# Hybrid decoder layer: later beta and decay products, later offers of two kinds of transposes, a residual transposed without its norm, and another clock for the planner's tasks

## The chip, the cores and the metric

The kernel runs on one core of one Trainium2 chip. The metric is the device time of one execution, in microseconds (us). The time before is a median of 981.6 us over three runs (980.06, 981.60 and 982.82).

## The reference, cut to what matters

One layer of a decoder over 512 tokens of width 1024, in float32: two token mixers side by side (retention and a gated delta rule), merged by gates, and then a gated feed-forward net with a causal convolution over three tokens.

```python
u = rmsnorm(h, g_mix)                                   # h: 512 x 1024
proj = u @ w_in                                         # 1024 x 9232
(rq, rk, rv, rgate, dq, dk_, dv_, dz, db, da, gate_r, gate_d) = split(proj)
...
g = -exp(dn_a_log) * softplus(da + dn_dt_bias)          # decay of each token and head
beta = sigmoid(db)                                      # step of the delta rule
do = gated_delta_chunkwise(cq, ck, cv, g, beta)         # 8 heads, chunks of 128 tokens
do = do * rsqrt(mean(do * do) + EPS) * dn_norm_g
y_dn = (do * silu(dz)) @ w_dn_br
merged = sigmoid(gate_r) * y_ret + sigmoid(gate_d) * y_dn
h = h + merged @ w_o

u2 = rmsnorm(h, g_ffn)                                  # (h * r) * g_ffn, one r per token
up = causal_dwconv(u2 @ w_up, ffn_conv_w) + ffn_conv_b  # 1024 x 5632, three taps
a, b = split(up, 2)
h = h + (silu(a) * b) @ w_down                          # 2816 x 1024
out = rmsnorm(h, g_final)
```

The factor r of the second rmsnorm belongs to a token. The products with w_up treat every token by itself, so r can be applied before them or after them; it has to be applied before the convolution, which mixes tokens.

## The kernel before, in words

**Numbers.** Every large product is made of three TensorE products in the fp32r type: each operand is split into a rounded part (hi) and the rest (lo), and hi·hi, lo·hi and hi·lo are summed (`mm3`, L387). ScalarE makes the hi part, VectorE the lo part (`weights`, L351, for a block of weights; `split`, L532, for an activation). The five square products of the mixer and the product with w_down go through Strassen's scheme in Winograd's form, with seven products of quarters in place of eight (`product`, L449; `PRODUCTS`, L62).

**Layout.** Activations that enter a product stand with channels on the 128 partitions and the 512 tokens in a row. Where a result has tokens on the partitions, TensorE transposes four 128x128 pieces of it into one PSUM bank against the identity (`transpose4`, L544).

**Order of the work.** TensorE's stream is written out by `body`, product by product. All else (evictions, norms, splits, transposes, the scans of the two mixers) is written as small tasks, Python generators. A class `Order` (L98 to L148) plans while the program is built: it has a clock, which every product moves on (`product`, L124), and for each other engine the time at which it is free (`issue`, L114). After each group of three products `poll` (L132) takes the tasks whose time has come, lets each issue its next step, and puts it back into the queue with a new time: the end of what it issued, plus a hop of 0.3 us (`HOP`), plus what the task itself yields. So a task that yields 0.6 is offered 0.6 us later than it could be. `hold` (L145) moves the clock on until something is planned to be ready. Each engine then runs its instructions strictly in the order in which this planner wrote them; semaphores keep the data right whatever the real times are. An instruction that comes too early in the order makes its engine wait, with everything that is queued behind it.

**Stages, in time.** (1) To 24 us: loading x, splitting it (`g_split`, L602), the squares of x for the first norm (`square`, `row_scales`, L615 to L649), and the first two weight blocks (`first_blocks`, L1257), which loop over eight k-tiles of 128 channels: three products into `pk`, three into `pq`, and two into `pba`, the 16 columns of w_in that give beta and the decays. `ba_w`, the split of those columns, is made by `ba_split` (L666). The norm of x is not applied to x: the products are scaled afterwards by `R`, a tile with the norm of each token in every partition (`scaled`, L1276). R comes from a product of ones with a diagonal tile (L637 to L646). `decays` (L708) makes beta and the decays from `pba`. (2) To 311 us: the products for keys, queries and values, with the fronts of the heads, retention, and the delta rule of heads 0 to 3. `solve_up` (L972) builds the inverses by small products, `scan` (L1026) runs over chunks, `scan_end` (L1080) norms the output of a head and transposes it (tile `pot`). (3) To 415 us: the products `pz` for the output gates, and the delta rule of heads 4 to 7. (4) To 578 us: four Strassen products (`matrix`, L1462): two gates, two branches. `m_out` (L1413) transposes the merged rows (tile `pmt`) and makes operands of them. (5) To 623 us: the product with w_o (`o_product`, L1555), whose results `o_into` (L1513) adds into the residual `h1`, eight tiles of 128x512. When both halves of a token tile are complete, it takes their squares on ScalarE, the sum on VectorE (`row_scale`, L526), the inverse root on GpSimd, and multiplies the two halves by it (one on ScalarE, one on VectorE, tile `hs`); `u2_out` and `u2_split` (L1537, L1544) transpose them (tile `pt`) and split them into u2hi and u2lo. (6) To 867 us: 44 blocks of w_up, alternately `pa` and `pb`; `ffn_conv` (L1574) reads each PSUM bank three times, once on ScalarE and twice on VectorE; `ffn_a` and `ffn_b` gate. The first three blocks run in halves, with tokens 256 to 511 first (`dense_c_halves`, L402). (7) To the end: the product with w_down (`down`, L1694), the last norm (`into`, L1659) and the output.

GpSimd issues the DMAs that add up weight quarters in memory (`presum`, L315), paced by a small pair of instructions on ScalarE and GpSimd (`pace`, L333). SyncE loads the weights (`fetch`, L288).

Of the kernel before, what the change touches and what calls it, by code (L numbers as in the profile page):

```python
# [19 lines left out]
P = 128  # L20
# [77 lines left out]
class Order:  # L98
# [15 lines left out]
    def issue(self, engine, us, banks=()):  # L114

        at = self.clock if self.now is None else self.now
        at = max(at, self.free.get(engine, 0.0))
        for b in banks:
            at = max([at, *(t + self.HOP for e, t in self.banks.get(b, {}).items() if e != engine)])
        self.done = self.free[engine] = at + us  # L120
        for b in banks:
            self.banks.setdefault(b, {})[engine] = self.done

    def product(self, us):  # L124
        self.clock += us
# [112 lines left out]
def body(nc, tc, ctx, io):  # L238
# [32 lines left out]
    def v3(ap, n=4):  # L271
        return ap.rearrange("p (n f) -> p n f", n=n)
# [807 lines left out]
    def scan_end(hd, o, ssqo):  # L1080
        h = hd["h"]
        ms = s4("mso")
        vec.tensor_scalar(ms, ssqo, 1.0 / P, EPS, ALU.mult, ALU.add)
        r = s4("ro")
        yield
        rsqrt(r, ms)
        yield
        vec.tensor_tensor(v3(o), v3(o), bc(r), ALU.mult)
        hd["got"].add("o")
        yield PW  # L1090
        pt = transpose4(o, "pot")
        yield
        d = S(f"doT{h}")
        act.activation(d, pt, AF.Identity, scale=prm[:, P_DG:P_DG + 1])
        doT[h] = d
# [158 lines left out]

    pba = PS("pba")

    def first_blocks():  # L1257

        pss = [PS(n) for n in ("pk", "pq")]
        ws = [tuple(v3(a, KT) for a in w) for w in first_w]  # L1260
        for k in range(KT):
            hold(lambda: k in g_ready)
            for i, ps in enumerate(pss):
                hold(lambda: (i, k // 4) in first_ready)
                mm3(ps, ws[i][0][:, k], ws[i][1][:, k], ghi[k], glo[k], k == 0, k == KT - 1)
                poll()
            hold(lambda: "ba" in first_ready)
            for j, x in enumerate(gx):
                pe.matmul(pba[:32], ba_w[:, k], x[k], start=(k + j == 0), stop=(k + j == KT))
            poll()  # L1270
        for i in range(2):
            spawn(weights(), 0.1 + 8.0 * i)
        spawn(decays(pba), 0.2)
        return pss
# [136 lines left out]
        o_opnd[name, t] = hi, lo  # L1411

    def m_out(t, i, r):  # L1413
        yield 0.2
        pt = transpose4(r, "pmt")
        yield
        name, half = f"B{i + 1}{t // 2 + 1}", t % 2
        m = o_raw[name, half] = S(f"mr{t}{i}")
        act.copy(m, pt)
        yield  # L1420
        if name != "B12":
            spawn(o_split(name, half, m))
        if name == "B12":
            t3 = S("mt3")
            vec.tensor_tensor(t3, o_raw["B22", half], m, ALU.subtract)
            t2 = o_raw["T2", half] = S("mt2")
            vec.scalar_tensor_tensor(t2, t3, -1.0, o_raw["B11", half], ALU.mult, ALU.subtract)
            spawn(o_split("T2", half, t2), 0.2)
            yield 0.5
            t1 = S("mt1")  # L1430
            vec.tensor_tensor(t1, o_raw["B11", half], m, ALU.subtract)
            spawn(o_split("T1", half, t1), 0.2)
            spawn(o_split("T3", half, t3), 0.2)
        elif name == "B21":
            while o_now[0] < 3:
                yield 0.5
            t4 = S("mt4")
            vec.scalar_tensor_tensor(t4, o_raw["T2", half], -1.0, m, ALU.mult, ALU.subtract)
            spawn(o_split("T4", half, t4), 0.2)
# [68 lines left out]

    u2hi = [S(f"u2hi{k}", F32R) for k in range(KT)]
    u2lo = [S(f"u2lo{k}", F32R) for k in range(KT)]  # L1510
    ssqs = [s4("ssq1", 2) for _ in range(NT)]

    def o_into(t, i, ps, op, last=False):  # L1513

        vec.tensor_tensor(h1[t][i], h1[t][i], ps, op)
        yield
        if not last:
            return
        junk = S("junk")
        act.activation(junk, h1[t][i], AF.Square, scale=1.0 / 32.0, accum_out=ssqs[t][:, i:i + 1])  # L1520
        if i == 0:
            return
        yield
        rr = s4("rr", 1)
        yield from row_scale(ssqs[t], rr)
        yield
        for i2 in range(2):
            xs = S("hs")
            if i2:
                vec.tensor_scalar(xs, h1[t][i2], rr, None, ALU.mult)  # L1530
            else:
                act.activation(xs, h1[t][i2], AF.Identity, scale=rr)
            spawn(u2_out(t, i2, xs), 0.6 * (i2 + 1))

    u2_ready = set()

# [35 lines left out]


    def ffn_conv(ps, ci):  # L1574
        w = prm[:, P_FW + 3 * ci:P_FW + 3 * ci + 3]
        acc = S2("acc")
        act.activation(acc, ps, AF.Identity, scale=w[:, 2:3], bias=prm[:, P_FB + ci:P_FB + ci + 1])
        yield
        for j in (1, 0):
            s = 2 - j  # L1580
            vec.scalar_tensor_tensor(acc[:, s:], ps[:, :T - s], w[:, j:j + 1], acc[:, s:], ALU.mult, ALU.add)
        yield
        return acc
# [215 lines left out]
```

## Time and profile before

| what | value |
|---|---|
| median of the runs | 981.6 us |
| the profiled execution: its own time | 980.2 us |
| its span, from the first to the last instruction | 978.3 us |
| outside the span | 1.9 us |
| mean granted TensorE clock | 0.999 |
| TensorE matmuls, busy | 963.4 us, 98% of the span |
| TensorE weight loads, busy | 804.6 us, 82% |
| VectorE, busy | 748.2 us, 76% |
| ScalarE, busy | 529.1 us, 54% |
| GpSimd, busy | 165.1 us, 17% |
| chain of work that ended last, TensorE's part | 85% |

In the profile's rows PE is TensorE's matmuls, PEld its weight loads, DVE VectorE, ACT ScalarE, POOL GpSimd and SP the engine that issues most DMAs. Most operations carry the line of a helper (L200 for all engines but TensorE, L230 and L235 for TensorE), so they are told apart by their tiles, written out<-in. A row of the timeline has the start and the duration in us, the engine, the operation, the tiles, the shape, and in brackets the idle time of the engine ahead of it with what ended it. A matmul of 512 columns shows 0.39 us, but the next one starts 0.23 us later, since matmuls overlap in the array; steps from start to start tell TensorE's pace. The pages' busy share of TensorE hides this overlap, so what matters is how long it stood idle, and for whom.

### The profile page before, as it was taken

How to read it: one execution, taken by the hardware profiler on the slowest of the kernel's cores; microseconds unless marked ns; L12 is line 12 of the kernel's file. 1: busy time of each engine (PE TensorE's matmuls, PEld its weight loads, DVE VectorE, ACT ScalarE, POOL GpSimd, SP SyncE). 2: the span in 40 equal slices, each digit the busy share in tenths (PEclk: the TensorE clock that was granted, in tenths of full speed). 3: DMA queues.
4: the chain of work that ended last, by engine and by line, in shares of the span. 5: the costliest groups of instructions: out<-in, count | busy, mean ns of one | idle time of the engine just before them, and what ended most of it. 6: DMA issues, size and time to landing. Idle time of an engine off the chain costs nothing.

```text
span 978.3 us, 14091 instructions
## 1 busy us (share of the span) xinstructions
PE 963.4 (98%) x5133; PEld 804.6 (82%) x5133; DVE 748.2 (76%) x1359; ACT 529.1 (54%) x1110; POOL 165.1 (17%) x209
## 2 busy tenths in 40 slices
PE   8999999999999999999999999899999999999997
PEld 6888888788888888978888887788888888888886
DVE  6888898567888898585899799865555676688785
ACT  6598222256955323586686646854344434356663
POOL 0121322224344020132000000221122221000001
PEclk9999999999999999999999999999999999999999
DMA  8244569958797695579976855666579998346663
GB/s 277 83 126 143 168 197 215 275 143 214 214 210 215 182 229 147 144 207 270 256 229 197 281 154 160 208 211 217 193 204 213 227 201 195 91 143 191 192 202 118
DMA packets 82949, 189.27 MB, mean 193 GB/s; under 512 B 22912, under 2 KB 31680, under 8 KB 82880
## 3 DMA queue, kind: packets, MB, share of 16 engines
q1 hardware_dynamic: 55360, 123.36, 39.4%
q0 software_dynamic: 27520, 65.02, 29.9%
q8 instruction: 40, 0.66, 0.3%
q14 instruction: 29, 0.24, 0.1%
HBM read 185.17 MB, written 68.19 MB: 259 GB/s over the span
## 4 chain that ended last, share of the span: by engine, by line
PE 85%; DVE 6%; ACT 4%; DMA 2%; issue 2%; POOL 0%; SPq 0%; POOLq 0%; DVEq 0%; ACTq 0%
PE pb L230 12%; PE pa L230 12%; PE py L230 12%; PE pd L230 10%; PE pz L230 9%; PE pr L230 9%; PE pq L230 3%; PE pv L230 3%; PE psc L230 3%; PE pk L230 3%; DVE wlo L200 2%; PE po L230 2%; PE pro L230 1%; ACT whi L200 1%; PE pm L230 1%
## 5 line engine op out<-in xcount | busy, mean ns | idle before, releaser
L200 ACT CAST whi<-wraw 128x1024 fp32r<-128x1024 f32 (+1 forms) x214 | 219.9, 1029 | 184.9 <-PE pr L230 54.2
L200 DVE TENSOR_TENSOR wlo<-wraw,whi 128x1024 fp32r<-128x1024 f32 (+1 forms) x214 | 255.3, 1194 | 63.7 <-ACT whi L200 63.1
L200 POOL TENSOR_SCALAR tock<-tick 128x1 f32<-128x1 f32 x72 | 34.0, 472 | 399.6 <-ACT tick L200 399.6
L200 DVE SCALAR_TENSOR_TENSOR acc<-pb,prm,acc 128x511 f32<-128x511 f32 (+1 forms) x44 | 33.0, 749 | 57.0 <-ACT acc L200 56.2
L230 PE MATMUL pa<-u2lo,whi 128*128 128x512 f32 (+1 forms) x192 | 71.4, 372 | 0.0
L230 PE MATMUL pa<-u2hi,whi 128*128 128x512 f32 (+1 forms) x192 | 71.4, 372 | 0.0
L230 PE MATMUL pa<-u2hi,wlo 128*128 128x512 f32 (+1 forms) x192 | 71.3, 371 | 0.0
L230 PE MATMUL pb<-u2hi,whi 128*128 128x512 f32 (+1 forms) x184 | 70.0, 380 | 0.0
L230 PE MATMUL pb<-u2lo,whi 128*128 128x512 f32 (+1 forms) x184 | 69.9, 380 | 0.0
L230 PE MATMUL pb<-u2hi,wlo 128*128 128x512 f32 (+1 forms) x184 | 69.9, 380 | 0.0
L230 PE MATMUL py<-whi,oh 128*128 128x512 f32 x160 | 62.9, 393 | 0.0
L230 PE MATMUL py<-wlo,oh 128*128 128x512 f32 x160 | 62.3, 390 | 0.0
L230 PE MATMUL py<-whi,ol 128*128 128x512 f32 x160 | 62.3, 389 | 0.0
L230 PE MATMUL pd<-whi,T 128*128 128x512 f32 (+1 forms) x198 | 55.3, 366 | 0.0
L230 PE MATMUL pz<-ghi,whi 128*128 128x512 f32 x128 | 51.4, 402 | 0.0
L230 PE MATMUL pr<-whi,ghi 128*128 128x512 f32 x128 | 51.1, 399 | 0.0
L230 PE MATMUL pr<-whi,glo 128*128 128x512 f32 x128 | 50.0, 390 | 0.0
L230 PE MATMUL pz<-ghi,wlo 128*128 128x512 f32 x128 | 49.9, 390 | 0.0
L230 PE MATMUL pz<-glo,whi 128*128 128x512 f32 x128 | 49.9, 390 | 0.0
L230 PE MATMUL pr<-wlo,ghi 128*128 128x512 f32 x128 | 49.9, 390 | 0.0
L200 DVE SCALAR_TENSOR_TENSOR acc<-pa,prm,acc 128x511 f32<-128x511 f32 (+1 forms) x44 | 33.0, 749 | 19.0 <-ACT acc L200 18.2
L200 ACT ACTIVATE acc<-pb,prm 128x512 f32<-128x512 f32 x22 | 17.2, 780 | 48.5 <-PE pb L230 48.5
(331 smaller groups left out, 2416.2 us busy)
## 6 DMA issues: line engine op xcount, KB each, us to landing
wraw<-w SPq DMA_DIRECT2D x98, 512.0 KB, 4.8
s<-wm POOLq DMA_DIRECT2D x30, 1024.0 KB, 8.2
wraw<-s SPq DMA_DIRECT2D x60, 512.0 KB, 3.8
s<-wd POOLq DMA_DIRECT2D x24, 704.0 KB, 5.5
wraw<-wm SPq DMA_DIRECT2D x30, 512.0 KB, 4.5
s<-s POOLq DMA_DIRECT2D x10, 1024.0 KB, 11.8
wraw<-wd SPq DMA_DIRECT2D x15, 512.0 KB, 3.6
s<-s POOLq DMA_DIRECT2D x8, 704.0 KB, 9.4
```

The lines of the kernel that those rows point to most:

```text
L200: return f(out, *args, **kw)
L230: self.engine.matmul(out, lhsT, rhs, start=start, stop=stop, **kw)
```

## The change

Five edits. First, `Order.issue`: a task's next time is now counted from the latest end of all that its step issued, where before it was the end of what it issued last. Second, the two products of beta and the decays for a k-tile are issued two k-tiles later, and those of the last two k-tiles after the loop. Third, `scan_end` yields 2.4 in place of 0.6 ahead of its transposes for heads 4 to 7, and `m_out` 1.6 in place of 0.2. Fourth, the residual is transposed as it is, right after its last addition; its squares are collected for all token tiles, and `o_scales` makes one tile R2 with the norm of each token. Fifth, `ffn_conv` first multiplies each of the 44 product banks by R2 into a tile of its own, and the convolution reads that tile.

```diff
@@ Order.issue
-        self.done = self.free[engine] = at + us
+        self.free[engine] = at + us
+        self.done = max(self.done or 0.0, at + us)
         for b in banks:
-            self.banks.setdefault(b, {})[engine] = self.done
+            self.banks.setdefault(b, {})[engine] = at + us
@@ scan_end
-        yield PW
+        yield PW if h < GH else 2.4
         pt = transpose4(o, "pot")
@@ first_blocks
+    def ba_part(k):
+        hold(lambda: "ba" in first_ready)
+        for j, x in enumerate(gx):
+            pe.matmul(pba[:32], ba_w[:, k], x[k], start=(k + j == 0), stop=(k + j == KT))
+        poll()
...
-            hold(lambda: "ba" in first_ready)
-            for j, x in enumerate(gx):
-                pe.matmul(pba[:32], ba_w[:, k], x[k], start=(k + j == 0), stop=(k + j == KT))
-            poll()
+            if k > 1:
+                ba_part(k - 2)
+        for k in range(KT - 2, KT):
+            ba_part(k)
@@ m_out
-        yield 0.2
+        yield 1.6
         pt = transpose4(r, "pmt")
@@ o_into and after it
-        if not last:
-            return
-        junk = S("junk")
-        act.activation(junk, h1[t][i], AF.Square, scale=1.0 / 32.0, accum_out=ssqs[t][:, i:i + 1])
-        if i == 0:
-            return
-        yield
-        rr = s4("rr", 1)
-        yield from row_scale(ssqs[t], rr)
-        yield
-        for i2 in range(2):
-            xs = S("hs")
-            if i2:
-                vec.tensor_scalar(xs, h1[t][i2], rr, None, ALU.mult)
-            else:
-                act.activation(xs, h1[t][i2], AF.Identity, scale=rr)
-            spawn(u2_out(t, i2, xs), 0.6 * (i2 + 1))
+        if last:
+            spawn(u2_out(t, i, h1[t][i]))
+            spawn(o_square(t, i), 2.0)
+
+    def o_square(t, i):
+        junk = S("junk")
+        act.activation(junk, h1[t][i], AF.Square, scale=1.0 / 32.0, accum_out=ssq2[:, i, t:t + 1])
+        yield
+        squared.append((t, i))
+        if len(squared) == 2 * NT:
+            yield from o_scales()
+
+    def o_scales():
+        ms, rr = s4("ms2"), s4("rr2")
+        vec.scalar_tensor_tensor(ms, ssq2[:, 0], EPS, ssq2[:, 1], ALU.add, ALU.add)
+        yield
+        rsqrt(rr, ms)
+        yield
+        diag = S("diag")
+        vec.tensor_tensor(v3(diag), ident.unsqueeze(1).to_broadcast([P, NT, P]), bc(rr), ALU.mult)
+        yield
+        ps = PS("pR")
+        pe.matmul(ps, ones, diag, start=True, stop=True)
+        yield
+        R = S("R2")
+        act.copy(R, ps)
+        yield
+        scale2.append(R)
@@ ffn_conv
+        while not scale2:
+            yield 0.3
         w = prm[:, P_FW + 3 * ci:P_FW + 3 * ci + 3]
+        x = S("scaled")
+        vec.tensor_tensor(x, ps, scale2[0], ALU.mult)
+        yield
+        ps = x
         acc = S2("acc")
         act.activation(acc, ps, AF.Identity, scale=w[:, 2:3], bias=prm[:, P_FB + ci:P_FB + ci + 1])
```

More of the change, by code (lines that the diff above doesn't have):

```diff
@@ L1510, in body @@
     u2lo = [S(f"u2lo{k}", F32R) for k in range(KT)]
-    ssqs = [s4("ssq1", 2) for _ in range(NT)]
+    ssq2 = const.tile([P, 2, NT], F32, name="ssq2")
+    squared = []
+    scale2 = []
     def o_into(t, i, ps, op, last=False):
```

## The prediction

> **What bounds the kernel now.** I read the page first, then the waits of TensorE, then the timeline around each of these waits, and last the windows of the stages that the change loads.
>
> ```profile
> span 978.3 us, 14091 instructions
> PE 963.4 (98%) x5133; PEld 804.6 (82%) x5133; DVE 748.2 (76%) x1359; ACT 529.1 (54%) x1110; POOL 165.1 (17%) x209
> ```
>
> The page says that TensorE (PE) is never far from work: 98% of the span against 76% for VectorE (DVE). So an edit gains only what TensorE stops waiting, and loses only what it newly waits or does. The list of TensorE's own waits is short enough to be read whole:
>
> ```profile
> PE pt L235 <- ACT hs L200: 2.0, 2, 1.6
> PE pba L230 <- DVE ba_w L200: 1.7, 1, 1.7
> PE pot L235 <- DVE vtok L200: 1.2, 1, 1.2
> PE pm L230 <- DVE m L200: 0.8, 1, 0.8
> PE po L230 <- DVE wlo L200: 0.8, 1, 0.8
> PE pt L235 <- DVE hs L200: 0.7, 1, 0.7
> PE pqt L235 <- ACT q L200: 0.4, 1, 0.4
> ```
>
> The columns are total us, times, longest. Four of these lie where the change works: pba (beta and decays), pot (head outputs), pt (the residual, twice), and pm, which the new rule for tasks touches. They sum to 2.0 + 1.7 + 1.2 + 0.8 + 0.7 = 6.4 us, the most that the edits can take away, before what they add.
>
> **Beta and decays two k-tiles later.** Sixteen products move, none is added.
>
> ```profile
> 7.87 0.72 ACT L200 ACTIVATE ghi<-xt,prm 128x512 fp32r<-128x512 f32 x1 [1.04 <-DMA xt<-xt]
> 8.62 0.75 DVE L200 SCALAR_TENSOR_TENSOR glo<-xt,prm,ghi 128x512 fp32r<-128x512 f32 x1 [1.07 <-ACT ghi L200]
> 9.77 0.42 PE L230 MATMUL pba<-ghi,ba_w 128*32 128x512 f32 x1 [1.65 <-DVE ba_w L200]
> 20.62 0.69 DVE L200 TENSOR_TENSOR sq<-sq 128x512 f32<-128x512 f32 x1
> 21.07 0.40 PE L230 MATMUL pba<-glo,ba_w 128*32 128x512 f32 x1
> 654.92 5.44 PE pb L230 x24
> ```
>
> The last row gives TensorE's pace: 5.44 / 24 = 0.227 us a product. Before, two pba products run from 9.77 and k-tile 1 follows at 9.77 + 0.45 = 10.22. Without pba ahead, k-tile 1 waits for its own lo part, which ends at 8.62 + 0.75 = 9.37; its first product needs only the hi part (8.59), so the stream stands as if it had begun at about 9.2. The two products must still run later: the gain is 10.22 - 9.2 - 0.45 = 0.6 us, not 1.65. Even that is not sure. The eight small products for x's norm need the last sum of squares, which DVE ends at 20.62 + 0.69 = 21.31, just when TensorE ends the pba product of 21.07 (21.30). A TensorE that is 0.6 ahead waits there, unless the planner lists those eight later in the stream. And the wait for q (0.4, above) hangs on the decays, which hang on this norm. I take 0.3 of the bounds 0 to 0.6.
>
> **Tasks go on when their later operation ends.** This bites only where a step issues on two engines. In `pace` and in the last norm the two ends are within a few tenths, so I cost those at nothing. In `solve_up` a step issues 32 small products and then a copy on ScalarE, which the planner held to end before the products did; so it listed DVE's negation m, and the 32 products after it, right behind:
>
> ```profile
> 192.49 1.15 PE L230 MATMUL pm<-tt,A 64*64 64x64 f32 x32
> 193.69 0.69 DVE L200 TENSOR_SCALAR m<-pm 128x512 f32<-128x512 f32 x1 [2.17 <-PE pm L230]
> 194.44 1.22 PE L230 MATMUL pm<-m,ta 64*64 64x64 f32 x32 [0.80 <-DVE m L200]
> ```
>
> TensorE stands idle from 193.64 to 194.44 while DVE negates. With the step counted to the end of its products, the second set is offered after m (0.69) and two hops, and key products fill the place. I take the whole 0.8; the bounds are 0 and 0.8. DVE waited 2.17 for m, and the retention's tiles queued behind it get ahead, which costs nothing.
>
> **Transposes offered later.** No instruction is added, only the place in TensorE's stream.
>
> ```profile
> 433.35 1.28 DVE L200 TENSOR_TENSOR vtok<-vtok,ro 128x512 f32<-128x512 f32 x2
> 434.08 0.66 PE L235 MATMUL pot<-cst,vtok 128*128 128x128 f32 x4 [1.16 <-DVE vtok L200]
> 554.33 0.40 PE L230 MATMUL py<-wlo,oh 128*128 128x512 f32 x1
> 554.78 0.66 PE L235 MATMUL pmt<-cst,res 128*128 128x128 f32 x4
> 598.17 1.22 DVE L200 TENSOR_TENSOR wlo<-wraw,whi 128x1024 fp32r<-128x1024 f32 x1
> 599.48 0.47 PE L230 MATMUL po<-wlo,mT 128*128 128x512 f32 x1
> ```
>
> pot waits 1.16 for DVE's vtok. Offered 1.8 us later, eight products (1.8 / 0.227) fill that time, so the wait goes: 1.2, bounds 0 and 1.2. Its reader is the branch operand of a much later product. For pmt the list shows no wait; one start comes 554.78 - 554.33 = 0.45 after the product ahead of it in place of 0.23, so its 1.4 us bring 0.2 (bounds 0 and 0.2). They also push the operands of the w_o product back. That region is tight: the weight split of 598.17 ends at 599.39, and TensorE uses it at 599.48, 0.09 later. If the operands of the later quarters come 1.4 later and this split stays queued behind them on DVE, TensorE pays up to 1.4. If the planner lists the split ahead of them, it pays nothing; it could even gain if the split moves up, but no row shows that its earlier end would be used. I take a loss of 0.4.
>
> **The residual without its norm.** Removed: four hs on ScalarE, four on DVE, four inverse roots on GpSimd (POOL). Added: one root of four columns, a diagonal on DVE, one product, one copy.
>
> ```profile
> L200 DVE TENSOR_SCALAR hs<-h,rr x4: 475/478/486, 617.6 to 632.0; 128x512 f32<-128x512 f32 x4
> 616.45 1.22 DVE L200 TENSOR_TENSOR wlo<-wraw,whi 128x1024 fp32r<-128x1024 f32 x1
> 616.61 1.49 POOL L200 TENSOR_TENSOR rr<-rs,mhalf 128x1 f32<-128x1 f32 x1 [0.68 <-DVE rs L200]
> 626.16 1.62 POOL L200 TENSOR_TENSOR rr<-rs,mhalf 128x1 f32<-128x1 f32 x1
> 628.59 1.09 PE L235 MATMUL pt<-cst,hs 128*128 128x128 f32 x8 [1.55 <-ACT hs L200]
> 973.55 0.55 POOL L200 TENSOR_TENSOR rr<-sm,mhalf 128x1 f32<-128x1 f32 x1 [4.00 <-DVE sm L200]
> 23.06 1.02 POOL L200 TENSOR_TENSOR rrx<-msx,mhalf 128x4 f32<-128x4 f32 x1 [22.56 <-DVE msx L200]
> 25.76 0.86 PE pss L230 x2
> 585.00:621.00 36.00, 34.11 (x156) 27.16 (x155) 33.98 (x51) 25.15 (x46) 2.07 (x2) 1.00 0.57 176
> ```
>
> The path at 628.59 runs DVE sum, POOL root, ScalarE hs, transposes. With the raw residual there is only DVE's addition ahead of the transposes, and the first three blocks of w_up in halves (72 products of half length, 72 x 0.227 / 2 = 8.2 us) cover the last token tiles. So 1.55 goes whole. Of the earlier 0.45 (2.0 - 1.55) and 0.7, DVE's load decides: it is busy 33.98 of 36 us from 585 to 621. The change frees two hs there (2 x 0.48) but brings the splits of u2 forward into the same stretch. I take all of 2.7 from the list, then pay 0.86 for the product that spreads the norms (the same product in stage 1 took 0.86) and 0.2 for waiting on its diagonal: 2.7 - 0.9 - 0.2 = 1.6. The wait's bounds are 0 and 1.1, since the root took 0.55 alone and 1.62 at the worst (1.02 for four columns). At best the 0.8 wait for wlo goes too, 2.7 + 0.8 - 0.9 = 2.6; at worst only 1.55 goes and the diagonal is late, 1.55 - 0.9 - 1.1 = -0.4.
>
> The 1.49 us root runs beside a DVE weight split with both inputs in SBUF (616.45 to 617.67); the 0.55 us root ran with DVE idle. The Trainium skill, page "SBUF — State Buffer", section "SBUF: two separate sides", states that such a DVE instruction and a GpSimd one that reads SBUF exclude each other for a whole instruction; the trace agrees. By that rule a root that meets a split comes up to 1.2 us later, and the sum below would be 2.5 in place of 3.7.
>
> **R2 in front of each convolution.** Forty-four DVE multiplications, and 88 others that now read a tile instead of a bank.
>
> ```profile
> L200 DVE TENSOR_TENSOR scaled<-pk,R 128x512 f32<-128x512 f32 x8 | 5.5, 682 | 1.7 <-PE pk L230 1.7
> L200 ACT ACTIVATE acc<-pa,prm 128x512 f32<-128x512 f32 x22 | 17.2, 780 | 46.1 <-PE pa L230 46.1
> 640.00:860.00 220.00, 220.00 (x988) 182.83 (x987) 140.35 (x194) 92.38 (x145) 39.30 (x58) 1.00 0.75 194
> 760.00:860.00 100.00, 100.00 (x443) 82.81 (x442) 68.55 (x102) 37.48 (x56) 15.24 (x20) 1.00 0.79 174
> ```
>
> The same operation in stage 2 took 682 ns: 44 x 0.68 = 30 us of DVE. From 640 to 860 TensorE has no idle time and DVE is busy 140.35 of 220; some 40 blocks add 27, so 76%. TensorE's own work hides it, and I cost it at nothing. The banks come free earlier, after one reader. If the cover fails, the price is that of the slower rival.
>
> **The sum.** 0.3 (start) + 0.8 (tasks) + 1.2 (pot) + 0.2 - 0.4 (pmt) + 1.6 (residual) + 0 (convolution) = 3.7. The profiled execution took 980.2 (span 978.3 and 1.9 around it), so 976.5 by its own time. It lies 1.4 below the median of the runs, 981.6, so as a median 977.9. The best ends give 0.6 + 0.8 + 1.2 + 0.2 + 2.6 = 5.4 (976.2), the worst without a new bound -1.4 - 0.4 = -1.8 (983.4). A measurement of this kernel tells 0.3%, some 2.9 us, from no change.
>
> **The rivals.**
>
> *DVE keeps the stretch around the w_o product.* For it: 33.98 of 36 us, and a split used 0.09 us after its end. Against it: DVE loses the multiplications there. Then pmt costs 1.4 and the residual gives 0: 0.3 + 0.8 + 1.2 + 0.2 - 1.4 = 1.1, a median of 980.5. Chance 0.17.
>
> *The early gains are taken back before 540.* From the start to 434 I count 2.3. If DVE's queue sets the pace in the branch products, a TensorE that comes earlier waits there.
>
> ```profile
> 480.00:540.00 60.00, 60.00 (x266) 49.70 (x265) 58.61 (x91) 43.32 (x64) 1.53 (x2) 1.00 0.71 211
> ```
>
> DVE is busy 58.61 of 60 us, which speaks for it; that TensorE is busy for all 60 and waits for nothing speaks against it, as the work is triggered by its own progress. It would leave 3.7 - 2.3 = 1.4, a median of 980.2. Chance 0.12.
>
> *VectorE becomes the bound in the feed-forward blocks (slower).* Per pair of blocks (10.88 us) the second half of the stage has DVE busy 0.6855 x 10.88 = 7.46 and idle 3.42. The multiplications take 1.36 of that, leaving 2.06. They also put a round trip on DVE's ordered queue: DVE multiplies, ScalarE makes acc (0.78), DVE goes on. If DVE finds nothing listed in between, it stands about 0.9 per block, 1.8 a pair: still covered. From 1.03 per block on, TensorE pays. At 1.5 it would be 3.0 - 2.06 = 0.94 a pair, 10.3 us over the eleven pairs of the second half, a median of 988.2. Against it: weight splits (one per block) are there to fill the trip. Chance 0.09.
>
> *The edits only move the waits.* A new order of the same tasks meets other late producers, and the sum is near nothing, 981. Chance 0.02.
>
> **How the numbers follow.** The forecast, 977.9, has 0.60. The two rivals that end within 0.3% and the last one together have 0.31, the slower one 0.09. The forecast's own range is 976.2 to 979.5. The range for 8 in 10 takes in the two rivals at 980.2 and 980.5 and most of the worst sum, and a microsecond below the best for the spread of the runs (980.06 to 982.82): 975.0 to 982.8.
>
> **What would show it.** Right: the pba wait gone and at most a smaller one at the norm's products near 21; no wait at the second pm and at pot; pt without waits; one matmul pair on R2's bank with a short wait; no wait of TensorE between 640 and 860, with DVE near 76% there. Wrong: TensorE's waits for wlo or mT between 585 and 621 larger than 0.8; pqt's wait grown by what the start gave; any wait of TensorE for wlo or a bank in the w_up blocks.

## The result, and the profile after

The kernel after takes 974.3 us (median of four runs, 973.99 to 974.47) against 980.83 (980.02 to 982.82) for the kernel before in the same session: a ratio of 0.993, 95% interval 0.9908 to 0.9952, or 6.5 us less. The prediction had the direction and the place (TensorE's waits), but gave 3.7 us and a range that ended at 975.0. The profiled execution's own time is 974.47, its span 972.7. Part of the miss is the base: the prediction counted down from 981.6, a median of three runs; a fourth, of 980.02, brings it to 980.83.

First the page of the kernel after, then all waits of TensorE (total us, times, longest):

```profile
span 972.7 us, 14171 instructions
PE 963.5 (99%) x5135; PEld 804.3 (83%) x5135; DVE 775.2 (80%) x1397; ACT 528.9 (54%) x1107; POOL 168.1 (17%) x206
```

```profile
PE warm L231 <- DVE mhalf L201: 1.1, 1, 1.1
PE pq L231 <- ACT doT L201: 1.1, 1, 1.1
PE pqt L236 <- ACT q L201: 0.6, 1, 0.6
PE pq L231 <- ACT whi L201: 0.2, 1, 0.2
PE pk L231 <- DVE glo L201: 0.2, 1, 0.2
```

VectorE has 27.0 us more work (775.2 - 748.2), TensorE as much as before. From TensorE's list the waits for pba, for vtok at pot, for m at pm and all three for hs at pt are gone, and, not forecast, the one for wlo at po. So is a wait of 0.3 for tt at psc, which the prediction's list left out (with the 1.1 of warm, the same in both). One of some size is new: the products pq wait for doT, ScalarE's copies of the transposed heads.

To see where the time went, compare the starts of the same product in both traces. From the timeline of TensorE before (first pv, first pz, first po, last po, first pd):

```profile
24.21 0.39 PE L230 MATMUL pv<-ghi,whi 128*128 128x512 f32 x1
...
310.97 0.48 PE L230 MATMUL pz<-ghi,whi 128*128 128x512 f32 x1
...
578.50 0.62 PE L230 MATMUL po<-whi,mB 128*128 128x512 f32 x2
...
622.59 0.39 PE L230 MATMUL po<-wlo,mT 128*128 128x512 f32 x1
...
866.92 0.61 PE L230 MATMUL pd<-whi,B 128*128 128x512 f32 x2
```

and the same five after:

```profile
23.10 0.39 PE L231 MATMUL pv<-ghi,whi 128*128 128x512 f32 x1
...
310.08 0.49 PE L231 MATMUL pz<-ghi,whi 128*128 128x512 f32 x1
...
576.72 0.62 PE L231 MATMUL po<-whi,mB 128*128 128x512 f32 x2
...
619.18 0.39 PE L231 MATMUL po<-wlo,mT 128*128 128x512 f32 x1
...
861.47 0.61 PE L231 MATMUL pd<-whi,B 128*128 128x512 f32 x2
```

The differences of neighbouring starts are the lengths of five stages. The table has them for these two kernels and for every kernel of the experiments, worked out in the same way from each one's trace; it is read down a column. (How well a stage repeats is seen in rows with the same instructions there: the last two within 0.1 us, pv to pz within 0.3, pz to po within 0.6. The first one repeats least: ScalarE started on the second tile of x between 6.57 and 7.87 us in these executions, whatever the kernel.)

| kernel | to pv | pv to pz | pz to po | po | last po to pd | median us |
|---|---|---|---|---|---|---|
| before | 24.21 | 286.76 | 267.53 | 44.09 | 244.33 | 980.83 |
| after | 23.10 | 286.98 | 266.64 | 42.46 | 242.29 | 974.3 |
| tasks' rule alone | 23.00 | 286.94 | 267.76 | 44.10 | 245.49 | 981.51 |
| beta later alone | 23.45 | 286.64 | 266.21 | 44.09 | 244.33 | 978.96 |
| later offers alone | 24.00 | 286.88 | 265.83 | 42.98 | 244.33 | 977.19 |
| residual alone | 23.78 | 286.70 | 268.24 | 43.59 | 242.31 | 976.89 |
| after, pmt early again | 23.12 | 286.75 | 267.98 | 43.67 | 242.29 | 976.8 |
| after, old rule | 23.55 | 287.12 | 266.23 | 42.52 | 242.28 | 973.88 |
| after, beta in place | 23.63 | 286.35 | 266.44 | 42.53 | 242.28 | 974.8 |
| after, pot early again | 22.80 | 286.78 | 267.76 | 42.49 | 242.30 | 975.34 |
| after, normed residual | 23.16 | 286.83 | 267.26 | 42.95 | 245.49 | 978.86 |
| after, R2 applied twice | 22.99 | 286.96 | 267.07 | 42.52 | 242.28 | 975.18 |
| after, R2 four times | 23.53 | 287.08 | 267.24 | 42.48 | 264.72 | 1003.65 |
| after, pot of heads 0 to 3 spread | 22.80 | 285.52 | 266.80 | 42.47 | 242.30 | 973.1 |
| the last, with the old rule | 23.66 | 285.86 | 266.25 | 42.50 | 242.30 | 972.84 |
| tasks' rule alone, pace as before | 23.41 | 286.29 | 267.77 | 44.12 | 244.32 | 979.37 |

So the change gains 1.1 before pv (about 0.6 of it because x came earlier: its second ghi starts at 7.27 in place of 7.87), loses 0.2 to pz, gains 0.9 to po, 1.6 in the product with w_o and 2.0 between there and pd, and from pd on nothing moves (0.15). That is 5.5 in all, and the two spans differ by 5.6. The other 0.9 of the 6.5 lies in no stage: the profiled execution before took 980.2, which is 0.6 under its kernel's median, and the one after 974.47, which is 0.2 over. The w_up blocks cost nothing, as forecast. The kernels of an experiment ran beside runs of the kernel before, whose medians there were 980.64 (the edits alone), 980.57 and 980.0 (edits undone, R2, spread) and 980.17 (the last two rows); the ratios below refer to these. These medians of one kernel differ by up to 0.8, and two rows with the same order of products (after, and R2 applied twice) by 0.9; so a difference under 1 us between two rows rests on the stages and the waits, not on the medians. One execution of the spread kernel, 3444 us long, was disturbed and is left out.

Three places deserve their rows. First, the new wait, from the timeline of the kernel after around 248 us:

```profile
243.98 2.47 ACT L201 ACTIVATE gb<-gb,nG 128x128 f32<-128x128 f32 x8
...
245.80 1.97 PE L236 MATMUL pot<-cst,vtok 128*128 128x128 f32 x16
...
246.46 1.28 ACT L201 ACT_TABLE_LOAD   x1
...
247.75 1.15 ACT L201 ACTIVATE gb<-gb 128x512 f32<-128x512 f32 x2
...
248.81 2.40 ACT L201 ACTIVATE doT<-pot,prm 128x512 f32<-128x512 f32 x4
...
249.53 0.50 PE L231 MATMUL pq<-ghi,whi 128*128 128x512 f32 x1 [1.05 <-ACT doT L201]
```

TensorE transposes all four heads in one go into four banks; ScalarE's queue has the decay tiles gb, and between them a table load of 1.28 us, ahead of the four copies. So the first bank is read only at 248.81, and the next product finds none free (an experiment below tests this). In the kernel before, the same transposes stood apart, at 240.18, 241.31, 244.52 and 247.04; gb and the load stood ahead of ScalarE's first copy there too, and TensorE waited for none. Second, the stretch of the w_o product; before:

```profile
602.96 0.62 ACT L200 CAST mT<-mt 128x512 fp32r<-128x512 f32 x1 [1.88 <-DVE mt L200]
...
603.49 1.04 ACT L200 CAST whi<-wraw 128x1024 fp32r<-128x1024 f32 x1
...
604.72 0.50 PE L230 MATMUL po<-wlo,mT 128*128 128x512 f32 x1 [0.77 <-DVE wlo L200]
```

after:

```profile
599.91 1.06 ACT L201 CAST whi<-wraw 128x1024 fp32r<-128x1024 f32 x1 [1.66 <-PE po L231]
...
600.87 1.13 ACT L201 CAST mT<-mt 128x512 fp32r<-128x512 f32 x2
```

Before, the weight cast stood behind an mT that waited 1.88 us for VectorE, and TensorE paid. After, the cast is ahead of both mT. Third, the product that spreads the norms, and the windows of the w_up blocks (us, then busy time and count of PE, PEld, DVE, ACT, POOL, then PEclk, DMA share, GB/s):

```profile
627.59 1.05 POOL L201 TENSOR_TENSOR rr<-ms,mhalf 128x4 f32<-128x4 f32 x1 [0.28 <-DVE ms L201]
...
628.67 0.69 DVE L201 TENSOR_TENSOR diag<-cst,rr 128x512 f32<-128x512 f32 x1 [1.17 <-POOL rr L201]
...
629.99 1.02 PE L231 MATMUL pR<-diag,ones 128*128 128x512 f32 x2
630.45 0.68 PE L231 MATMUL pa<-u2hi,whi 128*128 128x256 f32 x1
630.97 0.28 PE L231 MATMUL pa<-u2lo,whi 128*128 128x256 f32 x1
```

```profile
640.00:855.00 215.00, 215.00 (x950) 178.03 (x949) 163.78 (x231) 92.62 (x142) 46.58 (x56) 1.00 0.75 195
```

The pR pair has no wait. It sets TensorE back by 630.97 - 629.99 less one half product (0.12), that is 0.86, the price of the prediction. VectorE is busy for 163.78 of 215 us, 76%, also as forecast.

### The profile page after: what moved, and what is told of

Read it like the earlier page. It is cut to its first block, busy times and chain, and to the rows that moved or that the text cites. A ratio compares the mean times of both kernels' runs of the same rounds, so it can differ in the third digit from the quotient of the medians.

```text
span 972.7 us, 14171 instructions
## 1 busy us (share of the span) xinstructions
PE 963.5 (99%) x5135; PEld 804.3 (83%) x5135; DVE 775.2 (80%) x1397; ACT 528.9 (54%) x1107; POOL 168.1 (17%) x206
## 4 chain that ended last, share of the span: by engine, by line
PE 91%; ACT 4%; DVE 3%; issue 1%; DMA 1%; SPq 0%; POOLq 0%; POOL 0%; DVEq 0%; ACTq 0%
PE py L231 14%; PE pa L231 12%; PE pb L231 12%; PE pd L231 10%; PE pz L231 9%; PE pr L231 9%; PE po L231 4%; PE pq L231 3%; PE pv L231 3%; PE psc L231 3%; PE pk L231 3%; PE pro L231 1%; PE pm L231 1%; DVE wlo L201 1%; ACT gb L201 1%
## 5 line engine op out<-in xcount | busy, mean ns | idle before, releaser
L201 POOL TENSOR_SCALAR tock<-tick 128x1 f32<-128x1 f32 x72 | 40.5, 563 | 534.3 <-ACT tick L201 534.3
L201 DVE SCALAR_TENSOR_TENSOR acc<-scaled,prm,acc 128x511 f32<-128x511 f32 x88 | 65.6, 747 | 1.6
L201 DVE TENSOR_TENSOR scaled<-pb,R 128x512 f32<-128x512 f32 x22 | 15.2, 690 | 36.3 <-PE pb L231 36.3
L231 PEld LDWEIGHTS pa<-u2hi,whi 128*128 128x128 f32 x192 | 36.2, 189 | 6.5 <-issue 0.2
```

The lines of the kernel that those rows point to most:

```text
L201: return f(out, *args, **kw)
L231: self.engine.matmul(out, lhsT, rhs, start=start, stop=stop, **kw)
```

## The experiments: each edit alone

Four kernels add one edit each to the kernel before. **The rule for tasks:**

```diff
-        self.done = self.free[engine] = at + us
+        self.free[engine] = at + us
+        self.done = max(self.done or 0.0, at + us)
```

> Only the new rule for a task's next time, in the kernel before. Theory A (each edit acts where it sits): TensorE's 0.8 us wait for m near 194 and the 0.3 at the next psc go, and the new 1.1 us wait for doT near 249 appears here already, since it comes from the later place of the inverses; the sum is near nothing, -0.5 to +0.3 us. Theory B (the wait for doT comes from the other edits): no wait near 249, and TensorE ends 1.0 to 1.3 us earlier. Both: the 0.8 wait for wlo near 604 stays.

Measured: 981.51 us, ratio 1.0014 (1.0003 to 1.0026), a little slower. From its list of TensorE's waits:

```profile
PE pt L236 <- ACT hs L201: 3.2, 3, 1.6
...
PE pot L236 <- ACT doT L201: 1.1, 1, 1.1
...
PE po L231 <- DVE wlo L201: 0.8, 1, 0.8
```

The waits at pm and psc are gone, but doT is waited for in their place (pv to pz is 286.94 against 286.76), and at the residual's transposes a third wait for hs makes the last stage 1.16 longer. Theory A is right on the waits for m, psc, doT and wlo, but neither theory had the third hs, so the sum, 0.9 by the medians, lies outside both. The term of 0.8 for this edit did not arrive.

**Beta and decays later:**

```diff
-            hold(lambda: "ba" in first_ready)
...
+            if k > 1:
+                ba_part(k - 2)
```

> Only the later products of beta and the decays, in the kernel before. Theory A: the first products of pv start 0.5 us earlier, counted from the landing of x's second tile, because half of the 1.1 seen with all edits came from that tile landing 0.6 earlier in that execution; the wait at pqt near 77 takes back up to 0.4 of it; the whole kernel is 0.1 to 0.5 us faster. Theory B: the whole 1.1 us belongs to the edit and remains at the end.

Measured: 978.96, ratio 0.9988 (0.9978 to 0.9997). The wait at pba is gone; but so are those at pm, psc and pot, none of which this edit touches, and the one for doT is there. Moving a few products at the start shifts the planner's clock, and the places where a task is offered fall otherwise for 400 us. That is why pz to po gained 1.3 here. Ahead of pv the edit alone gave nothing: pv starts 0.8 earlier, but so does the second ghi (7.04). A wait of 0.4 for the last sum of squares at the norm's products near 21 took the gain back, as the prediction feared; the kernel after has no such wait. The 1.7 us by the medians lie outside both theories.

**The two later offers:**

```diff
-        yield PW
+        yield PW if h < GH else 2.4
...
-        yield 0.2
+        yield 1.6
```

> Only the two later offers of transposes (pot 2.4, pmt 1.6), in the kernel before. Theory A: the 1.2 us wait at pot near 434 shrinks to about 0.1, the short start at pmt goes (0.2), and the 0.8 us wait for wlo near 604 goes too, because the later pmt puts a weight split ahead of a cast that waits; sum -2.0 us. Theory B (my step on record): the wait for wlo stays or grows by up to 1.4; sum -1.4 to 0.

Measured: 977.19, ratio 0.997 (0.9959 to 0.9981). pz to po is 1.7 shorter (the pot wait is gone), and the w_o stage 1.1: whi goes ahead of mT, as in the kernel after, and the wait for wlo is gone. The waits at pm and pt stay. That is theory A's mechanism; the gain, 3.5 by the medians and 3.0 by the spans (978.3 and 975.3), is more than its 2.0.

**The residual and R2:**

```diff
+        if last:
+            spawn(u2_out(t, i, h1[t][i]))
+            spawn(o_square(t, i), 2.0)
...
+        vec.tensor_tensor(x, ps, scale2[0], ALU.mult)
```

> Only the raw residual, the one tile of norms and its multiplication ahead of the convolution, in the kernel before. Theory A: the three waits at pt (2.7 us) go, the product for the tile adds 0.9, the wait for wlo near 604 stays; sum -1.8 to -2.4 us, none of it lost between 640 and 860. Theory B (the residual edit is also what removed the wait for wlo): that wait goes too, and the sum is -3.0 to -3.7 us.

Measured: 976.89, ratio 0.9969 (0.9958 to 0.9981). The w_o stage is 0.5 and the last one 2.0 shorter, 2.5 together, all waits at pt gone. The reordering brings one new wait, pmt for res, which lengthens pz to po by 0.7, and leaves wlo's, as theory A said:

```profile
PE po L230 <- DVE wlo L200: 0.8, 1, 0.8
PE pmt L235 <- DVE res L200: 0.7, 1, 0.7
```

The spans (978.3 and 975.9) gain 2.4, theory A's top; the medians gain 3.8, more than the stages of the profiled execution show.

## The experiments: one edit undone in the kernel after

**pmt offered early again:**

```diff
-        yield 1.6
+        yield 0.2
         pt = transpose4(r, "pmt")
```

> The kernel after with one edit undone: m_out yields 0.2 again ahead of its transposes. Theory A (the later pmt takes away the wait for wlo near 603, because ScalarE then casts a weight block, whi, ahead of the second mT): here the order is mT, mT, whi again, so a row of TensorE waiting for DVE wlo of 0.7 to 0.8 comes back between 585 and 621, TensorE stands 0.9 to 1.3 later from 605 on, and the median is 975.4 (974.9 to 975.9). Theory B (in the kernel after it is the raw residual, with ScalarE's and VectorE's hs gone, that took the wait away): no wait for wlo comes back, 974.3 within 0.3. The prediction's own term (pmt costs 0.4 net there) would have it at 973.9.

Measured: 976.8, ratio 0.9965 (0.9951 to 0.9978), 2.5 above the kernel after.

```profile
PE pmt L236 <- DVE res L201: 1.2, 1, 1.2
...
PE po L231 <- DVE wlo L201: 0.8, 1, 0.8
```

The w_o stage is 1.2 longer with the wait for wlo back, as theory A said, and a wait that no theory had, pmt for res, adds 1.3 ahead of it. So in this kernel undoing the later offer of pmt costs some 2.5 us, more than any other edit but the residual. Theory A has the wait for wlo, but by the second wait the median lies 0.9 above its range. Theory B and the prediction's own sign are out.

**The old rule for tasks** (the two lines of `Order.issue` as before):

```diff
-        self.done = max(self.done or 0.0, at + us)
+        self.done = self.free[engine] = at + us
```

> The kernel after with one edit undone: a task's next time is again counted from the end of what its step issued last. Theory A (the rule has no worth of its own by now: the wait for m goes with any shift of the order and the wait for doT at 249 comes in its place; what the rule cost alone, 1.2 us at the transposes of the normed residual, is gone with that residual): 974.3, between 973.8 and 974.9. Theory B (the prediction: the rule takes the 0.8 wait for m away): the wait for m at the second pm comes back with 0.7 to 0.8, 975.1. Theory C (the rule costs in the kernel after what it cost alone): 972.9, and no wait for doT near 250.

Measured: 973.88, ratio 0.9935 (0.9922 to 0.9947), not to be told from the kernel after. The wait for doT is there, none for m. Theory A: the rule has no worth here.

**Beta and decays back in their k-tile:**

```diff
-            if k > 1:
-                ba_part(k - 2)
+            for j, x in enumerate(gx):
+                pe.matmul(pba[:32], ba_w[:, k], x[k], start=(k + j == 0), stop=(k + j == KT))
```

> The kernel after with one edit undone: the two products of beta and the decays stand behind their own k-tile again. Theory A (the prediction's step: TensorE stood for pba, but the two products have to run later all the same): the wait of 1.6 to 1.7 for ba_w comes back at 9.5, TensorE starts its values' products (pv) 0.3 to 0.6 later against the start of its second k-tile's hi part, and the median is 974.7 (974.4 to 975.1). Theory B (the whole wait counts, and what follows meets other waits too): 976.0.

Measured: 974.8, ratio 0.9942 (0.993 to 0.9955).

```profile
PE pot L236 <- ACT doT L201: 1.0, 1, 1.0
PE pba L231 <- DVE ba_w L201: 0.7, 1, 0.7
```

pv comes 0.5 later, but there is no wait at pqt, which had 0.6 in the kernel after, and at pz this execution is 0.1 ahead. The median is near theory A's and far from B's; what is left of the start's gain behind pqt is 0 to 0.5, too little to settle against the scatter of x's landing. The wait for ba_w came back with 0.7, not with theory A's 1.6 to 1.7. Over the six profiled executions with the two products in their own k-tile it lies between 0.6 and 1.7, so the 1.7 in the profile of before was the largest.

**pot of heads 4 to 7 early again:**

```diff
-        yield PW if h < GH else 2.4
+        yield PW
```

> The kernel after with one edit undone: scan_end yields 0.6 again ahead of the transposes of heads 4 to 7. Theory A (the prediction's step: the wait for vtok is 1.2 and goes with the later offer): a row of TensorE waiting for DVE vtok of 1.2 to 1.4 comes back near 435, 975.5 (975.1 to 975.9). Theory B (any shift of the order takes that wait away, as it went with the earlier edits alone): no wait for vtok, 974.3 within 0.3.

Measured: 975.34, ratio 0.995 (0.9938 to 0.9962), theory A: the wait is back.

```profile
PE pot L236 <- DVE vtok L201: 1.4, 1, 1.4
```

pz to po is 1.1 longer, near the prediction's 1.2; rows with the order of the kernel after differ by 0.6 there, so the size is known no better.

**The normed residual again** (the parts of `o_into` and `ffn_conv` as before):

```diff
-            spawn(u2_out(t, i, h1[t][i]))
+            spawn(u2_out(t, i2, xs), 0.6 * (i2 + 1))
...
-        vec.tensor_tensor(x, ps, scale2[0], ALU.mult)
```

> The kernel after with the two edits of the residual undone: it is normed ahead of its transposes again, and the convolution reads the product banks. Theory A (the residual gives here what it gave alone, 2.5 at the transposes): waits for hs of 2.5 to 2.9 come back between 617 and 640, 976.8 (976.4 to 977.3). Theory B (in the normed residual the rule for tasks costs 1.2 on top, as it did alone): waits for hs of 3.5 or more, 978.0 (977.5 to 978.5).

Measured: 978.86, ratio 0.999 (0.998 to 1.0), so 4.6 above the kernel after; theory B came close, but the median lies 0.4 above its range and 0.9 above its figure.

```profile
PE pt L236 <- ACT hs L201: 3.1, 3, 1.6
...
PE pt L236 <- DVE hs L201: 0.7, 1, 0.7
...
PE py L231 <- ACT res L201: 0.6, 1, 0.6
```

The last stage is 3.2 longer and the w_o stage 0.5: 2.5 from the residual as it was alone, and the rule's 1.2 on top. The wait of 0.6 for res, near 450, is not the edit's: TensorE's order up to 608 us is that of the kernel after, and the two kernels with R2 applied twice and four times, in the same order, waited 0.3 and 0.4 there. It comes and goes between executions.

## The experiments: two disputed costs, and a burst spread out

**Where the rule alone loses 1.2 us.** The prediction had cost `pace` at nothing. In the kernel with the rule alone, `pace` keeps the old count:

```diff
         pool.tensor_scalar(tock, tick, 1.0, None, ALU.mult)
+        order.done = order.free["pool"]
```

> The kernel before with the rule for tasks alone, but in pace the next time is again counted from the end of GpSimd's part. In TensorE's stream this moves one thing against the rule alone: the last eight transposes of the normed residual (pt) stand twelve half products later, as in the kernel before. Theory A (the 1.2 us that the rule alone costs there comes from pace: its later turn puts a root ahead of a DMA on GpSimd, the planner offers the last transposes earlier, and they wait for hs, which stands behind eight copies u2hi on ScalarE): the third wait of 1.1 for ScalarE's hs is gone, and the median is 1.2 below the rule alone's 981.5: 980.3 (979.9 to 980.8). Theory B (the prediction: pace costs nothing, and the 1.2 comes from the tasks of the residual themselves): 981.5, with three waits for hs.

Measured: 979.37, ratio 0.9991 (0.9982 to 1.0).

```profile
PE pt L236 <- ACT hs L201: 2.1, 2, 1.6
```

The third wait is gone and the last stage is 244.32, as before the change; the only difference in TensorE's stream is the place of the last eight pt, a dozen half products later. Theory A, though the median lies 0.5 below its range (the kernel before, run beside it, is 0.5 lower too: 980.17 in place of 980.64): a planning rule that moves a tiny instruction pair by a fraction of a microsecond moved transposes ahead of their input. In the kernel after this costs nothing that can be told: no hs is left to wait for.

**VectorE's room in the w_up blocks.** The multiplication by R2 issued twice, and four times:

```diff
         vec.tensor_tensor(x, ps, scale2[0], ALU.mult)
+        vec.tensor_tensor(x, ps, scale2[0], ALU.mult)
```

> The kernel after, with the multiplication by R2 in front of each convolution issued twice (the second writes the same tile again; same output): 44 more VectorE instructions of 0.69 us, 30.4 us in all, 1.38 per pair of blocks. Theory A (the multiplication lies in VectorE's idle time, which is 2.2 of 10.88 us per pair in the second half and 3.0 in the first): still covered, 0.8 left per pair, TensorE without a wait from 640 to 860, VectorE at 85 to 88% there, median within 0.6 of 974.3. Theory B (the round trip on VectorE's ordered queue, which the slower rival priced, is already near its limit): TensorE waits for a bank or for wlo in the w_up blocks, 3 us or more, 977 or later.

> The kernel after, with the multiplication by R2 issued four times per block (three more, same output): 4.14 us more per pair of blocks. Theory A (VectorE becomes the bound once its idle time is used up): 4.14 - 2.16 = 1.98 over per pair in the second half (755 to 865, ten pairs: 20), 4.14 - 2.97 = 1.17 in the first (640 to 755, ten and a half pairs: 12), so 32 us, 1006 (1000 to 1012), VectorE over 95% busy there and TensorE waiting for banks or wlo. Theory B (VectorE's idle time cannot be used in full, because its ordered queue stands for ScalarE in each block): 1 to 2 us more per pair on top, 1020 to 1050. Theory C (there is more room than the windows show): under 995.

Measured: 975.18, ratio 0.9946 (0.9934 to 0.9959), with two; 1003.65, ratio 1.0238 (1.0224 to 1.0252), with four. The windows with two, then with four, and TensorE's waits with four:

```profile
640.00:855.00 215.00, 215.00 (x950) 178.09 (x949) 190.29 (x273) 94.96 (x142) 38.79 (x56) 1.00 0.76 195
```

```profile
755.00:855.00 100.00, 91.89 (x394) 72.76 (x393) 97.56 (x146) 35.78 (x53) 17.52 (x22) 1.00 0.80 175
```

```profile
PE pb L231 <- DVE wlo L201: 12.4, 16, 2.2
PE pd L231 <- DVE wlo L201: 3.6, 1, 3.6
```

With two, VectorE is busy 190.29 of 215 us (89%), and the stage takes 242.28 against 242.29: nothing lost. (The profiled execution is 0.3 longer than that of the kernel after, by the wait for res near 450 that comes and goes. The median is 0.9 longer, outside theory A's 0.6, and no stage shows a cause.) With four, VectorE stands at 97.6% and becomes the bound; the 29.3 us lost are within theory A's 26 to 38 over the kernel after. The fit is partly luck. The stage itself is 22.4 longer, less than theory A's figure, and 6.4 were lost behind it: the 3.6 at pd, and the granted clock, which the windows show at 0.50 from 879 to 882 us, 0.52 from 896 to 903, and again at 1.00 from 903 on. Each of these lies at one of the two longest stops for wlo (2.2 until 878.3 and 3.6 until 897.4); whether that is the reason was not tested. VectorE's idle time could be used almost in full, and in the kernel after and with two, the round trip to ScalarE that the slower rival feared costs nothing that TensorE sees.

**The new wait for doT.** The transposes of heads 0 to 3 one k-tile apart:

```diff
-        yield PW if h < GH else 2.4
+        yield 5.0 if h < GH else 2.4
```

> The kernel after with 5.0 in place of 0.6 as the yield ahead of the transposes of heads 0 to 3, which stands them one k-tile apart in TensorE's stream, in place of 16 transposes in one go. Theory A (the wait of 1.05 for doT at 249 comes from four PSUM banks that are filled at once while ScalarE is at the decay tiles gb ahead of them): with a bank at a time no product waits for doT, 973.2 (972.9 to 973.6), faster than the kernel after by 1. Theory B (ScalarE is late there whatever the order): another tile of ScalarE's (k, vtok or whi) is waited for in its place, 974.3 or later.

Measured: 973.1 (five executions, 972.87 to 974.19), ratio 0.9929 (0.9918 to 0.9941). All of TensorE's waits:

```profile
PE warm L231 <- DVE mhalf L201: 1.1, 1, 1.1
PE pqt L236 <- ACT q L201: 0.4, 1, 0.4
PE pk L231 <- ACT whi L201: 0.4, 1, 0.4
PE pss L231 <- DVE sq L201: 0.2, 1, 0.2
```

No wait for doT, and pv to pz is 1.5 shorter: theory A. ScalarE is no earlier (gb, the table load and now also a weight cast stand ahead of its first copy, at 249.19); what changed is that the banks fill one by one. With the old rule for tasks besides (the two lines as above):

> The kernel after with the transposes of heads 0 to 3 one k-tile apart (a yield of 5.0) and without the rule for tasks. Theory A (the rule has no worth of its own in the kernel after, and the wait for doT goes with the spread transposes under either rule): 973.2 (972.6 to 973.8), no wait for doT, no wait for m. Theory B (the rule is what keeps the second pm free of a wait once doT no longer holds the stream back): a wait for m of 0.7 to 0.8 comes back, 974.2.

Measured: 972.84, ratio 0.9924 (0.9911 to 0.9938). No wait for m comes back, so the rule isn't what keeps it away. The stage between pv and pz shows the gain plainly (1.5 and 1.1); by their intervals these two kernels can't be told from the kernel after as a whole, nor from each other.

## Why the prediction was wrong, point by point

*The frame held.* The time is TensorE's products and its waits; what the stages gained lies at waits that came or went, and the w_up blocks hid 30 us of new work on VectorE. All three rivals with a mechanism fell: the stretch around the w_o product got shorter, not longer; the 0.89 at pz and 1.78 at po (310.97 - 310.08, 578.50 - 576.72) were not taken back before 540; and VectorE takes twice the work that was added before TensorE pays. The fourth rival, that the edits only move the waits, was right in one place: the wait for doT came for those at pm and psc.

*The step that failed first: pmt, a loss of 0.4 against a gain of 0.2.* It gained 1.1 us: so much shorter is the w_o stage with the later offers alone, and undoing the offer in the kernel after makes it 1.2 longer. The prediction priced the delayed operands against a split used 0.09 us after its end, and set the gain from a split that moves up at nothing, because "no row shows that its earlier end would be used". A row did show it: the 0.8 for wlo in TensorE's own list. The prediction used that row, but at the wrong edit, in the best end of the residual's term; with the residual alone the wait stays, with the later offers alone it goes. Its cause was in the timeline, a weight cast queued behind an mT that waited 1.88 us. With the later offer the cast stands ahead of the mT. So the worst end of the pmt term (-1.4) had a mechanism, and the best end (0.2) missed the one that decided. The other 1.3 that undoing it costs, at pmt for res, was in no list of before, so it is no part of the 6.5; it appears when other edits shift the order (0.7 with the residual alone), and the later offer keeps it away.

*The residual, 1.6, was mis-sized.* It gave 2.5 alone. The product cost the 0.86 that was priced, the wait for its diagonal was 0 in place of 0.2, and the waits removed were worth more than their 2.7. The list counts a wait from the modelled end of the product ahead; from start to start the stop of 1.55 cost more:

```profile
626.76 0.28 PE L230 MATMUL pb<-u2hi,wlo 128*128 128x256 f32 x1
628.59 1.09 PE L235 MATMUL pt<-cst,hs 128*128 128x128 f32 x8 [1.55 <-ACT hs L200]
```

A step of 1.83 where half products step by 0.12 is 1.71 lost. With 0.16 more for each of three stops the waits are 3.2, less 0.86 is 2.3; the remaining 0.2 is not placed.

*The tasks' rule, 0.8, gave nothing*: the waits for m and tt, 1.1 together, went and 1.1 for doT came; pv to pz is 0.2 longer, as much as the wait at pqt grew. Its zero for `pace` was wrong by 1.2 in the kernel before; in the kernel after undoing the rule changes nothing that can be told. The wait at pm did go, but so it did with other shifts of the order ahead of it (it is gone with the beta edit alone, and in the kernel after without the rule), and the wait for doT stood ready to take its place.

*pot, 1.2, was about right*: 0.9 from pz to po, and 1.1 there when it is undone. *The start, 0.3*, fits: from the second ghi to pv it is 16.34 before and 15.83 after, a gain of 0.5. The wait at pqt, grown from 0.4 to 0.6, then takes back 0.2; the prediction's list has that as a sign of being wrong if it takes all that the start gave. *The convolution, nothing*, was right.

Put together, by the stages of the two kernels:

| term | forecast | found |
|---|---|---|
| start | 0.3 | 0.5 |
| tasks' rule (with pqt) | 0.8 | -0.2 |
| pot | 1.2 | 0.9 |
| pmt (0.2 - 0.4) | -0.2 | 1.1 |
| residual | 1.6 | 2.5 |
| sum | 3.7 | 4.8 |

To the 4.8 come 0.6 from x, which is luck, and the 0.9 of the medians that lies in no stage; that is near the 6.5. So the stages show the edits to give about 1.1 us more than forecast, with pmt and the residual too low by 1.3 and 0.9 and the tasks' rule too high by 1.0. The rest of the distance between 977.9 and 974.3 is not explained by any step: 0.8 is the base (from 980.83 the range would have ended at 974.2), and the rest is scatter between executions. The edits don't add up one by one, though: alone they gave -0.9, 1.7, 3.5 and 3.8 (each median against 980.64), because each one also moves the others' waits.

The Trainium skill's rule that the prediction weighed, page "SBUF — State Buffer", section "SBUF: two separate sides" (a GpSimd instruction that reads SBUF and a VectorE one with two SBUF inputs exclude each other), had nothing to act on here: the one root, 1.05 us, ran while VectorE stood idle for 1.17. Where a root of four columns does meet a split the traces agree with the rule: 1.91 us at 102.39 before (split from 102.21 to 103.43) and 1.95 at 420.95 after (split from 420.77 to 421.99), against 1.00 to 1.06 for most such roots without one. So the price of meeting a split was 0.9 there, where the prediction took up to 1.2.

## What to carry to other kernels

When an edit shifts the order in which an engine gets its instructions, one that waits holds up those queued behind it, as the mT here held the cast. So go through the whole list of waits of the engine that bounds the time and ask of each what instruction stands ahead of its producer, not only of the waits that the edit is meant for. Price a stop from start to start of the bounding engine's instructions, not by its listed idle time. Look at a long transpose burst that fills several banks at once while its reader has other work queued: the one here cost 1.05 us of waiting, and spread out, one bank at a time, nothing.

## What was unexpected of the hardware

The second tile of x comes by the same DMA in every kernel, and ScalarE started on it between 6.57 and 7.87 us in the profiled executions (7.87 before, 7.27 after, the latter behind a weight cast that had waited 0.81 for its own DMA); that is more than the gain looked for at the start. With VectorE at 89% of the stage, TensorE still lost nothing in 242 us. With four multiplications the granted clock fell to half for some 10 us in all, at the end of the stage that TensorE spent partly waiting and just behind it; before and after show no such stretch there.
